# The gated convolution's input projection: every pair of tiles from the fourth block on by seven products, and the sixth product moved to fourth place

## The chip, the cores and the metric

One core of one Trainium2 chip runs the whole program once. The metric is the device time of that execution in microseconds (us). Engines by the profile's names: PE (TensorE matmul), PEld (its weight load), DVE (VectorE), ACT (ScalarE), POOL (GpSimd), SP (SyncE, which issues most DMAs here).

## The reference, cut to what matters

The program is one step of a four-layer decoder trunk for 512 prompt tokens and 8 sample tokens, 520 columns in all. The change touches the second layer alone, the short gated convolution:

```python
def shortconv_mixer(h, w_in, conv_w, w_out, buf):
    u = h @ w_in                           # 1024 -> 4 * 2048
    bg, cg, xb, z = jnp.split(u, 4, axis=-1)
    cx = cg * xb
    cpad = jnp.concatenate([buf.astype(cx.dtype), cx], axis=1)
    y = conv_w[0] * cpad[:, 0:T]
    for j in range(1, CONV_W):             # CONV_W = 3
        y = y + conv_w[j] * cpad[:, j:j + T]
    out = (bg * y * jax.nn.silu(z)) @ w_out
    return out, cpad[:, -(CONV_W - 1):]
```

All arrays are float32.

## The kernel before, in words

**Two halves of a float32.** TensorE is fed rounded operands, so each operand is held as a high part and a low part (value minus high part). A product takes three matmuls: high by high, high by low, low by high. For a weight tile `wf` of 128x1024 (128 outputs, all 1024 inputs) `high` (L255) is an ACT copy to `wh`. `low` (L257 to L264) is made in one of two ways. Mostly it is a DVE subtraction to `wl` (L264). For the first weight of a *moved* item (`Item.moved`, all of the convolution's weights except four) ACT writes the negated high part into `wl` (L260), and a DMA on POOL's queue adds the weight itself from HBM (L262).

**A plain tile** (`proj`, `mm6`): eight blocks of inputs, each with three matmuls (L334, L336, L338) on each of the two parts of the 520 columns.

**A pair by seven** (`seven`): two tiles, each cut into two halves of its inputs (a, b), against the activations cut in two halves of 260 columns, make eight block products; by sums of weights and of activations the same result comes from seven. Each product is twelve matmuls (L362 to L364). The weight sums `s1`, `s2`, `s4`, and a fourth that goes back into the second tile's `wf`, are four POOL instructions of 128x512 (L276 to L279, op "sum"); each of the three sums is split again into a high part `hs` (ACT) and a low part `ls` (DVE). The activations' sums are made once for the stage. Results are put together from PSUM by DVE adds: L380 (u2), L389 (u3), L393 (two halves at once), L372 (last quarter), and by ACT copies (L377, L386).

The order of a pair's products on PE is 11, T2, T1, then the seventh product "22" of the *previous* pair (`last`, run by `flush`, L384), then 21, T3, T4. So a pair's own last result and what hangs on it (`done`) come in the window of the pair or plain tile after it. r1 and r6 (the PSUM places) are used twice in a pair: 11 then 21, T2 then T3.

**The blocks.** The stage has 16 blocks j of four tiles: xb and cx (w_b 32+j and 16+j), bg and z (w_b j and 48+j). Blocks 0 to 2 are plain. From block 3 (`NPLAIN`) on, the first pair (xb, cx) goes by seven; the second pair (bg, z) goes by seven in even blocks and as two plain tiles in odd ones (`paired`). The `done` of a first pair multiplies cx by xb (L1109), and then runs the convolution: an ACT scaling (L1071), DVE L1076 to L1079, and two small POOL copies (L1067, L1068). The `done` of a second pair is a Silu on ACT and L1115 on DVE; in a plain block the same is L1126 and an ACT call. L1083, the product with the gate, is issued a little later from a side stream (`gate`).

**What sets the order.** The order is written by hand (`manual_schedule`): the order in which the program issues instructions is the order on each engine. Weights are made ahead of their use by a plan. `plan` lists items (a tile, or a pair), and `due` gives each step of an item (load, load2, sum, high, low, high2, low2, and the s parts) a due time on a planned clock, in which a plain tile costs 5.76 and a pair 10.08. It counts on 4 slots each for `wf`, `wh` (with `wl`) and `hs` (with `ls`): `take` gives the time at which a slot comes free. While the matmuls are written, `pump` issues each step once the planned clock has passed its due time. A pair's products pump 1.44 each.

Of the kernel before, what the change touches and what calls it, by code (L numbers as in the profile page):

```python
# [39 lines left out]
NPLAIN = 3  # L40
# [13 lines left out]

def paired(j):

    return 0 if j < NPLAIN else 2 - j % 2


def plan():  # L60
# [25 lines left out]
    for j in range(16):  # L86
        for n, q in enumerate(((2, 1), (0, 3))):
            keys = [("w_b", 16 * u + j) for u in q]
            if n < paired(j):
                out.append(Item(*keys, cost=10.08))  # L90
            else:
                out.extend(Item(key) for key in keys)
# [21 lines left out]
def due(items):  # L114

    ops, t, seq = [], 0.0, 0
    slots = {"wf": [0.0] * FBUFS, "wh": [0.0] * HBUFS, "hs": [0.0] * SBUFS}

    def take(tag, until):
        free = slots[tag]  # L120
        at = min(free)
        free.remove(at)
        free.append(until)
        return at

    def at(time, i, op):
        nonlocal seq
        ops.append((time, seq, i, op))
        seq += 1
        return time  # L130

    for i, it in enumerate(items):
        it.begin = t
        if len(it.keys) == 1:
            ld = min(slots["wf"])
            sp = at(max(ld, take("wh", t + (it.life or it.cost))), i, "high")
            low = at(sp + 1.3, i, "low")
            at(take("wf", low + 2) - 0.01, i, "load")
        else:
            ld, ld2 = sorted(slots["wf"])[:2]  # L140
            one = at(max(ld, ld2, t - 12.8), i, "sum")
            h1 = at(max(ld, take("wh", t + 5.76), t - 14.4), i, "high")
            h2 = at(max(ld2, take("wh", t + 10.08), one + 6.6), i, "high2")
            low1 = at(h1 + 1.3 if it.moved else max(h1 + 1.3, one + 3), i, "low")
            low2 = at(max(h2 + 1.3, one + 3), i, "low2")
            at(take("wf", max(low1, one + 7) + 1) - 0.01, i, "load")
            at(take("wf", low2 + 3) - 0.01, i, "load2")
            for n, need, until in (("2", t - 6.8, t + 2.88), ("1", t - 4.8, t + 4.32), ("4", t - 2.0, t + 17.3)):
                h = at(max(take("hs", until), need, one + 3), i, "high" + "s" + n)
                at(h + 0.6, i, "lows" + n)  # L150
        t += it.cost
    return sorted(ops)
# [42 lines left out]
class Net:  # L195
# [145 lines left out]
    def seven(self, keys, B, dst, done):  # L341

        nc = self.nc
        mm = nc.tensor.matmul
        t = self.item(*keys)
        a, b = slice(0, 512), slice(512, 1024)
        r1, r6, v = self.aux()[:, :HALF], self.aux()[:, :HALF], self.psum()  # L350
        r4, r5 = v[:, :HALF], v[:, 512 : 512 + HALF]
        part = lambda n, cols=slice(0, 512): (t["h" + n][:, cols], t["l" + n][:, cols])
        halves = self.act(), self.act()
        s1, u2, u3 = halves[0][:, :HALF], halves[0][:, HALF:], halves[1][:, :HALF]
        add = nc.vector.tensor_add

        def product(out, w, name, start):
            for k in range(4):
                c = slice(k * P, (k + 1) * P)
                hi, lo = B[name][k]  # L360
                go = {} if start else {"skip_group_check": True}
                mm(out, w[0][:, c], hi, start=start and k == 0, stop=False, **go)  # L362
                mm(out, w[0][:, c], lo, start=False, stop=False, **go)  # L363
                mm(out, w[1][:, c], hi, start=False, stop=k == 3, **go)  # L364

        def step():
            self.pump(1.44)
            self.tick()

        def last():  # L370
            product(r5, part("s4"), "22", False)
            add(dst[0][:, HALF:], r5, u2)  # L372
            done()
            step()

        product(r1, part("1", a), "11", True)
        nc.scalar.activation(s1, r1, AF.Copy)  # L377
        step()
        product(r6, part("s2"), "T2", True)
        add(u2, r6, s1)  # L380
        step()
        product(r5, part("s1"), "T1", True)
        step()
        self.flush()  # L384
        product(r1, part("1", b), "21", False)
        nc.scalar.activation(dst[0][:, :HALF], r1, AF.Copy)  # L386
        step()
        product(r6, part("2", a), "T3", False)
        add(u3, r6, s1)  # L389
        step()  # L390
        product(r4, part("2", b), "T4", True)
        pair = lambda x, n: x.rearrange("p (u c) -> p u c", u=2)[:, :, :n]
        add(pair(dst[1], HALF), pair(v, HALF), u3.unsqueeze(1).broadcast_to([P, 2, HALF]))  # L393
        step()
        self.pend = last
# [6 lines left out]
    @staticmethod  # L402
    def part(ps, j, m=P):

        n = PARTS[j].stop - PARTS[j].start
        if isinstance(ps, tuple):
            return ps[j][:m, :n]
        return ps[:m, BASE + PARTS[j].start : BASE + PARTS[j].stop]
# [643 lines left out]
    def conv(self, h, lay):  # L1052
# [4 lines left out]
        with ExitStack() as st:  # L1057
# [45 lines left out]
            def block(j):  # L1103
                xb, cx, z = (self.act() for _ in range(3))
                bg = self.act() if paired(j) > 1 else None
                c = []

                def first():
                    nc.vector.tensor_mul(cx, cx, xb)  # L1109
                    c.extend(taps(j, cx))  # L1110
                    conv(j, cx, *c)

                def second():
                    nc.scalar.activation(z, z, AF.Silu)
                    nc.vector.tensor_mul(c[0], bg, c[0])  # L1115
                    self.gate.gens.append(times(c[0], z))

                self.seven((("w_b", 32 + j), ("w_b", 16 + j)), self.sums, (xb, cx), first)
                if j == 15:
                    self.gate.drain()  # L1120
                    self.gate.gens.extend(parts(n) for n in range(4))
                if paired(j) > 1:
                    self.seven((("w_b", j), ("w_b", 48 + j)), self.sums, (bg, z), second)
                else:
                    ps = self.proj("w_b", j, a=h)
                    nc.vector.tensor_mul(c[0], ps, c[0])  # L1126
                    ps = self.proj("w_b", 48 + j, a=h)
                    nc.scalar.activation(z, ps, AF.Silu)
                    self.gate.gens.append(times(c[0], z))
# [557 lines left out]
```

## Time and profile before

| | us |
|---|---|
| median of three runs | 2155.67 |
| lowest and highest | 2151.12 and 2155.94 |
| the profiled execution | 2155.09 |
| its span, first to last instruction | 2153.3 |
| PE busy in the span | 2129.6 (99%) |
| DVE, ACT, POOL busy | 1383.3, 898.8, 395.2 |

The span lies 1.8 us below the time of the same execution. The convolution's pairs by seven run from about 655 to 945 us in the trace. In that stretch the granted clock is 1.00 throughout, which is the upper level, 2.4 GHz. A window of a pair is the time from its first matmul to that of what comes after it. The examples below are neighbouring windows: 745.65 to 755.71 (the second pair of an even block), 755.71 to 765.77 (the first pair of the odd block after it), 765.77 to 779.54 (that block's two plain tiles, with the flushed product among them), and 779.54 to 788.16 (the next block's first pair, which has nothing to flush).

### The profile page before, as it was taken

What the parts mean: (1) busy time and instruction counts of PE and PEld (TensorE: products, weight loads), DVE (VectorE), ACT (ScalarE), POOL (GpSimd) and SP (SyncE); (2) the same over time, 40 slices, a digit from 0 to 9 for tenths busy, and PEclk for the clock granted to TensorE, in tenths of its full rate; (3) what the DMA queues carried; (4) which work ended last, traced back from release to release, by engine and by line L of the source; (5) the groups of instructions that cost most, each with busy time, mean ns of one, the idle gap of its engine ahead of it and who ended that gap; (6) DMA issues with size and microseconds to landing.
All of it is one profiled execution on the core that took longest, in us unless ns stands there. A gap on an engine that the chain in (4) does not pass through costs nothing.

```text
span 2153.3 us, 42675 instructions
## 1 busy us (share of the span) xinstructions
PE 2129.6 (99%) x17560; PEld 2111.6 (98%) x17560; DVE 1383.3 (64%) x3064; ACT 898.8 (42%) x1434; POOL 395.2 (18%) x487
## 2 busy tenths in 40 slices
PE   8999999999999999999999999999999999999998
PEld 8999999999999999999999999999999999999998
DVE  7677767653565766751478787777867466666434
ACT  6544444432355554554333333333334342222223
POOL 1111110100035545521014223222220000000000
PEclk9999999999999999999999999999999999999999
DMA  4644454322257666678343555555544332323321
GB/s 164 193 177 143 154 182 165 99 95 93 89 140 165 159 169 164 157 198 188 88 136 120 162 193 190 185 173 165 199 169 156 98 114 93 98 90 99 119 79 50
DMA packets 112951, 305.22 MB, mean 142 GB/s; under 512 B 34260, under 2 KB 38612, under 8 KB 110708
## 3 DMA queue, kind: packets, MB, share of 16 engines
q1 hardware_dynamic: 104404, 272.54, 38.9%
q0 software_dynamic: 8208, 29.89, 7.8%
q8 instruction: 138, 2.26, 0.4%
q14 instruction: 57, 0.47, 0.1%
q10 hardware_dynamic: 144, 0.06, 0.0%
HBM read 279.63 MB, written 22.82 MB: 140 GB/s over the span
## 4 chain that ended last, share of the span: by engine, by line
PE 83%; DVE 6%; DMA 4%; issue 2%; ACT 2%; POOL 2%; SPq 0%; POOLq 0%; DVEq 0%; ACTq 0%
PE ps L334 23%; PE ps L338 23%; PE ps L336 23%; DMA wl<-w_b 2%; PE ax L1334 1%; PE ax L334 1%; PE ax L338 1%; PE ax L336 1%; DVE wl L264 1%; PE ax L364 1%; PE ax L362 1%; PE ax L363 1%; ACT wh L255 1%; PE ax L943 1%; PE ps L362 1%
## 5 line engine op out<-in xcount | busy, mean ns | idle before, releaser
L334 PE MATMUL ps<-hi,wh 128*128 128x256 f32 x4672 | 963.1, 287 | 1.8 <-DVE a L485 0.8
L338 PE MATMUL ps<-hi,wl 128*128 128x256 f32 x4672 | 939.5, 282 | 2.3 <-DMA wl<-w_b 2.3
L336 PE MATMUL ps<-lo,wh 128*128 128x256 f32 x4672 | 939.2, 282 | 0.1
L334 PEld LDWEIGHTS ps<-hi,wh 128*128 128x128 f32 x4672 | 725.8, 188 | 7.5 <-issue 1.4
L338 PEld LDWEIGHTS ps<-hi,wl 128*128 128x128 f32 x4672 | 723.4, 188 | 3.5 <-DMA wl<-w_b 3.3
L336 PEld LDWEIGHTS ps<-lo,wh 128*128 128x128 f32 x4672 | 725.3, 188 | 0.3 <-DVE lo L800 0.3
L264 DVE TENSOR_TENSOR wl<-wf,wh 128x1024 fp32r<-128x1024 f32 x287 | 364.2, 1272 | 167.3 <-ACT wh L255 163.8
L255 ACT ACTIVATE wh<-wf 128x1024 fp32r<-128x1024 f32 x344 | 360.8, 1053 | 157.2 <-issue 92.0
L1211 POOL TENSOR_TENSOR a<-a,a 32x520 f32<-32x520 f32 x48 | 68.9, 1436 | 296.1 <-ACT a L502 98.9
L627 DVE TENSOR_TENSOR x<-ps,x 128x520 f32<-128x520 f32 x32 | 22.4, 699 | 121.7 <-PE ps L338 121.6
L489 ACT ACTIVATE a<-a 128x520 f32<-128x520 f32 x42 | 26.8, 639 | 155.2 <-DVE a L485 155.1
L502 ACT ACTIVATE a<-ps 128x520 f32<-128x520 f32 x42 | 47.3, 1127 | 99.0 <-PE ps L338 72.5
L1212 POOL TENSOR_TENSOR a<-a,a 32x520 f32<-32x520 f32 x48 | 65.3, 1360 | 122.1 <-DVE a L1210 112.6
L466 ACT ACTIVATE hi<-x 128x520 fp32r<-128x520 f32 x32 | 20.5, 640 | 156.3 <-DVE x L627 156.3
L264 DVE TENSOR_TENSOR ls<-a,hs 128x512 fp32r<-128x512 f32 x57 | 65.4, 1158 | 12.1 <-ACT hs L255 11.9
L485 DVE TENSOR_TENSOR a<-ps,a 128x520 f32<-128x520 f32 x85 | 58.9, 693 | 20.8 <-PE ps L338 17.4
L649 DVE TENSOR_TENSOR a<-ax,a 128x256 f32<-128x256 f32 (+1 forms) x62 | 23.7, 424 | 72.5 <-ACT a L647 72.5
L1237 ACT ACTIVATE S<-S,nmx 128x128 f32<-128x128 f32 (+1 forms) x96 | 40.0, 417 | 65.8 <-DVE nmx L1234 65.5
L459 DVE CUSTOM_DVE_ANT_0 kc<-kc,qb 128x128 f32<-128x128 f32 (+1 forms) x192 | 54.3, 340 | 13.7 <-DMA kc<-kc 13.7
L262 POOL DMA_DIRECT2D wl<-w_b x41 | 36.3, 885 | 144.5 <-ACT wl L260 139.1
L260 ACT ACTIVATE wl<-wh 128x1024 fp32r<-128x1024 f32 x57 | 60.1, 1058 | 1.4
L1499 POOL COPY pool_p<-xpad 128x15 f32<-128x15 f32 x16 | 3.1, 196 | 300.7 <-DVE xpad L485 300.7
(344 smaller groups left out, 2924.4 us busy)
## 6 DMA issues: line engine op xcount, KB each, us to landing
wf<-w_c SPq DMA_DIRECT2D x80, 512.0 KB
wf<-w_a SPq DMA_DIRECT2D x64, 512.0 KB
wf<-w_b SPq DMA_DIRECT2D x64, 512.0 KB
wl<-w_b POOLq DMA_DIRECT2D x41, 512.0 KB, 7.1
wf<-w_pg SPq DMA_DIRECT2D x32, 512.0 KB
wf<-w_d SPq DMA_DIRECT2D x32, 512.0 KB
pb<-scr_p SPq DMA_DIRECT2D x8, 1292.0 KB
Ci<-C_in SPq DMA_DIRECT2D x16, 512.0 KB
```

The source lines that it names most:

```text
L255: nc.scalar.activation(t["h" + k], t["w" + k], AF.Copy)
L260: nc.scalar.activation(t["l1"], f(t["h1"]), AF.Copy, scale=-1.0)
L264: nc.vector.tensor_sub(t["l" + k], t["w" + k], f(t["h" + k]))
L334: mm(out[j], wh, a[0][:, PARTS[j]], start=start, stop=False)
L336: mm(out[j], wh, a[1][:, PARTS[j]], start=False, stop=False)
L338: mm(out[j], wl, a[0][:, PARTS[j]], start=False, stop=stop)
L362: mm(out, w[0][:, c], hi, start=start and k == 0, stop=False, **go)
L459: self.nc.vector.tensor_tensor_reduce(junk, a, b, 1.0, 0.0, ALU.mult, ALU.add, out)
L485: nc.vector.tensor_mul(dst[:, :T], ps, self.r)
L502: nc.scalar.activation(dst, split(ps), AF.Copy)
L1211: nc.gpsimd.tensor_mul(b[:32], t[:32], cs[0])
L1212: nc.gpsimd.tensor_mul(a[:32], a[:32], cs[1])
```

## The change

Four edits. `paired` gives 2 for every block from the fourth on, so that in the seven odd blocks 3, 5, ... 15 bg and z are made by `seven` too (19 pairs become 26). In `seven`, the product T4, which was the last of the six, is issued right after the flush; the two DVE adds L389 and L393 then both stand behind T3. The plan keeps the pair's first weight in its slot for 8.64 instead of 5.76, since product 21, its last reader, now comes later. And the low part of a moved single tile is planned at the time of its high part, not 1.3 behind it.

```diff
 def paired(j):
-    return 0 if j < NPLAIN else 2 - j % 2
+    return 0 if j < NPLAIN else 2
...
         if len(it.keys) == 1:
             ld = min(slots["wf"])
             sp = at(max(ld, take("wh", t + (it.life or it.cost))), i, "high")
-            low = at(sp + 1.3, i, "low")
+            low = at(sp if it.moved else sp + 1.3, i, "low")
...
-            h1 = at(max(ld, take("wh", t + 5.76), t - 14.4), i, "high")
+            h1 = at(max(ld, take("wh", t + 8.64), t - 14.4), i, "high")
...
         self.flush()
+        product(r4, part("2", b), "T4", True)
+        step()
         product(r1, part("1", b), "21", False)
         nc.scalar.activation(dst[0][:, :HALF], r1, AF.Copy)
         step()
         product(r6, part("2", a), "T3", False)
         add(u3, r6, s1)
-        step()
-        product(r4, part("2", b), "T4", True)
         pair = lambda x, n: x.rearrange("p (u c) -> p u c", u=2)[:, :, :n]
         add(pair(dst[1], HALF), pair(v, HALF), u3.unsqueeze(1).broadcast_to([P, 2, HALF]))
```

POOL's queue before, in the middle of the stage; the names are `wl` for a low weight part that a DMA completes, `wf` for a loaded weight, `a` for a sum or an activation:

```order
L262 DMA wl_8337<-w_b 128x1024
L276 TENSOR_TENSOR a_8353<-wf_8230 128x512
L277 TENSOR_TENSOR a_8354<-a_8353,wf_8186 128x512
L278 TENSOR_TENSOR wf_8230<-wf_8186,wf_8230 128x512
L279 TENSOR_TENSOR a_8355<-wf_8186,a_8354 128x512
L1067 COPY cv_p<-a_8248 128x2
L1068 COPY cv_s<-a_8248 128x8
L262 DMA wl_8460<-w_b 128x1024
L262 DMA wl_8520<-w_b 128x1024
L262 DMA wl_8593<-w_b 128x1024
L276 TENSOR_TENSOR a_8610<-wf_8478 128x512
```

The same queue now, in the same part of the stage:

```order
L262 DMA wl_8378<-w_b 128x1024
L1067 COPY cv_p<-a_8249 128x2
L1068 COPY cv_s<-a_8249 128x8
L276 TENSOR_TENSOR a_8486<-wf_8358 128x512
L277 TENSOR_TENSOR a_8487<-a_8486,wf_8318 128x512
L278 TENSOR_TENSOR wf_8358<-wf_8318,wf_8358 128x512
L279 TENSOR_TENSOR a_8488<-wf_8318,a_8487 128x512
L262 DMA wl_8515<-w_b 128x1024
L276 TENSOR_TENSOR a_8619<-wf_8495 128x512
L277 TENSOR_TENSOR a_8620<-a_8619,wf_8455 128x512
```

The three DMAs in a row (one for a pair, two for plain tiles) are gone: every sum is followed by one DMA and every DMA by a sum, with the two small copies between them in every second window.

DVE's queue before, at the seam between an even block and the odd one after it:

```order
L264 TENSOR_TENSOR ls_9541<-a_9403,hs_9524 128x512
L380 TENSOR_TENSOR a_9553<-ax_9551,a_9553 128x260
L372 TENSOR_TENSOR a_9298<-ps_9416,a_9417 128x260
L1115 TENSOR_TENSOR a_9479<-a_9298,a_9479 128x520
L389 TENSOR_TENSOR a_9554<-ax_9551,a_9553 128x260
L1083 TENSOR_TENSOR a_9297<-a_9479,a_9297 128x520
L393 TENSOR_TENSOR a_9546<-ps_9552,a_9554 128x520
L372 TENSOR_TENSOR a_9545<-ps_9552,a_9553 128x260
L1109 TENSOR_TENSOR a_9546<-a_9546,a_9545 128x520
```

And now, from the window of a block's second pair on:

```order
L264 TENSOR_TENSOR ls_9186<-a_9028,hs_9166 128x512
L1083 TENSOR_TENSOR a_8790<-a_8987,a_8790 128x520
L380 TENSOR_TENSOR a_9195<-ax_9193,a_9195 128x260
L264 TENSOR_TENSOR ls_9239<-a_9160,hs_9235 128x512
L372 TENSOR_TENSOR a_9058<-ps_9064,a_9065 128x260
L1109 TENSOR_TENSOR a_9059<-a_9059,a_9058 128x520
L1076 SCALAR_TENSOR_TENSOR a_9257<-a_9059,cols,a_9257 128x511
L1077 SCALAR_TENSOR_TENSOR a_9257<-a_9059,cols,a_9257 128x510
L1078 SCALAR_TENSOR_TENSOR a_9257<-cv_in,cols,a_9257 128x8
L1079 SCALAR_TENSOR_TENSOR a_9257<-cv_in,cols,a_9257 128x8
L264 TENSOR_TENSOR wl_9263<-wf_9035,wh_9237 128x1024
L264 TENSOR_TENSOR ls_9281<-a_9159,hs_9267 128x512
```

L1083 now stands in the same window as L1109, ahead of it, between the low part of s4 and that of s2; the low part of s1 (the last row) stands behind the whole convolution.

## Rows read from the trace of the kernel before

**Rows 1.** The page: busy time by engine, granted clock in slices, chain by engine.

```profile
PE 2129.6 (99%) x17560; PEld 2111.6 (98%) x17560; DVE 1383.3 (64%) x3064; ACT 898.8 (42%) x1434; POOL 395.2 (18%) x487
...
PEclk9999999999999999999999999999999999999999
...
PE 83%; DVE 6%; DMA 4%; issue 2%; ACT 2%; POOL 2%; SPq 0%; POOLq 0%; DVEq 0%; ACTq 0%
```

**Rows 2.** Waits of PEld, 640 to 960 us: total us, times, longest us.

```profile
PEld ps L338 <- DMA wl<-w_b: 3.3, 5, 0.8
```

**Rows 3.** Timeline of PE: start us, us, line, operation, idle before.

```profile
755.71 0.28 PE L362 MATMUL ax<-hi,wh 128*128 128x260 f32 x1
...
765.77 0.40 PE L334 MATMUL ps<-hi,wh 128*128 128x256 f32 x2
...
766.95 0.51 PE L338 MATMUL ps<-hi,wl 128*128 128x256 f32 x2 [0.54 <-DMA wl<-w_b]
767.29 0.40 PE L334 MATMUL ps<-hi,wh 128*128 128x256 f32 x2
767.53 0.40 PE L336 MATMUL ps<-lo,wh 128*128 128x256 f32 x2
...
779.54 0.28 PE L362 MATMUL ax<-hi,wh 128*128 128x260 f32 x1
```

**Rows 4.** Windows: busy PE, PEld, DVE, ACT, POOL, then clock, DMA share, GB/s.

```profile
745.65:755.71 10.06, 10.06 (x86) 10.06 (x85) 7.49 (x8) 4.79 (x9) 7.11 (x7) 1.00 0.60 154
755.71:765.77 10.06, 10.06 (x86) 10.06 (x85) 6.02 (x12) 7.22 (x10) 1.75 (x2) 1.00 0.81 200
765.77:779.54 13.77, 13.23 (x110) 13.03 (x109) 10.17 (x13) 5.25 (x7) 8.09 (x9) 1.00 0.59 137
779.54:788.16 8.62, 8.62 (x74) 8.62 (x73) 6.31 (x7) 5.32 (x8) 5.34 (x4) 1.00 0.69 174
```

**Rows 5.** DVE's groups, 655 to 945 us: busy us, mean ns of one | idle before.

```profile
L264 DVE TENSOR_TENSOR ls<-a,hs 128x512 fp32r<-128x512 f32 x57 | 65.4, 1158 | 12.1 <-ACT hs L255 11.9
L264 DVE TENSOR_TENSOR wl<-wf,wh 128x1024 fp32r<-128x1024 f32 x19 | 24.0, 1264 | 1.1 <-ACT wh L255 1.1
...
L393 DVE TENSOR_TENSOR a<-ps,a 128x520 f32<-128x520 f32 x19 | 13.3, 700 | 8.2 <-PE ps L364 7.6
...
L1115 DVE TENSOR_TENSOR a<-a,a 128x520 f32<-128x520 f32 x6 | 4.2, 700 | 0.2
```

**Rows 6.** Timeline of DVE in the first window and just behind it.

```profile
746.47 2.63 DVE L264 TENSOR_TENSOR ls<-a,hs 128x512 fp32r<-128x512 f32 x1
...
751.96 0.42 DVE L372 TENSOR_TENSOR a<-ps,a 128x260 f32<-128x260 f32 x1
752.41 1.35 DVE L1109 TENSOR_TENSOR a<-a,a 128x520 f32<-128x520 f32 x1
...
757.54 0.68 DVE L264 TENSOR_TENSOR ls<-a,hs 128x512 fp32r<-128x512 f32 x1
```

**Rows 7.** Timeline of POOL, the same windows.

```profile
746.32 0.91 POOL L262 DMA_DIRECT2D wl<-w_b  x1 [3.42 <-ACT wl L260]
746.93 1.61 POOL L276 TENSOR_TENSOR a<-wf 128x512 f32<-128x512 f32 x1
748.62 1.62 POOL L277 TENSOR_TENSOR a<-a,wf 128x512 f32<-128x512 f32 x1
750.20 1.28 POOL L278 TENSOR_TENSOR wf<-wf,wf 128x512 f32<-128x512 f32 x1
751.44 1.75 POOL L279 TENSOR_TENSOR a<-wf,a 128x512 f32<-128x512 f32 x1
...
757.77 0.89 POOL L262 DMA_DIRECT2D wl<-w_b  x1 [3.63 <-ACT wl L260]
```

**Rows 8.** Timeline of ACT: the copy behind product 21, and an `hs` part.

```profile
754.95 0.37 ACT L386 ACTIVATE a<-ax 128x260 f32<-128x260 f32 x1
...
757.26 0.62 ACT L255 ACTIVATE hs<-a 128x512 fp32r<-128x512 f32 x1
```

**Rows 9.** The DMAs of L262 by source line, whole program.

```profile
DMA to landing us min/median/max: 5.4/7.1/9.9
```

**Rows 10.** The chain of waits, 752 to 768 us: start, us, what.

```profile
757.77 9.13 DMA wl<-w_b
```

## The prediction

> **What bounds the kernel now.** I read the page first. PE is busy for 2129.6 of 2153.3 us, the clock stands at its upper level in every slice, and 83% of the chain of waits lies on PE [rows 1]. So time goes only where PE does less work, or where a wait of PE goes. Next I read the waits of PE in the convolution's stretch, because the change is there alone. The only one of size is a plain tile's low weight part, which a DMA of POOL's queue completes: five waits of PEld, 3.3 us in all [rows 2]. Then the timeline of PE, for what each form costs. The first window, a pair by seven, runs from one L362 to the next stretch's first matmul: 755.71 to 765.77, 10.06 us, seven products of 1.44 [rows 3]. The two plain tiles with one flushed product take 765.77 to 779.54, 13.77 us. In them one wait can be seen: L334 at 767.29 is the fourth group of matmuls, which at the pace of 0.24 (767.29 to 767.53) would have begun at 766.49, so 0.80 is lost [rows 3]. Last I read DVE, POOL and ACT in the same windows, since the change takes 1.5 us from PE in each odd block and gives these engines more to do in it [rows 4 to 8].
>
> **PE's work.** Without its wait and the flushed product the plain stretch is 13.77 - 0.80 - 1.44 = 11.53 us. A pair costs 10.06. Each of the seven odd blocks saves 1.47: 10.3 us. The plain tiles' waits lie in these same blocks and go with them, if nothing takes their place: 3.3 us [rows 2]. The best case is 13.6 us, or 2155.1 - 13.6 = 2141.5 on the clock of the profiled run, which stands 0.6 below the median of the three.
>
> **DVE and POOL.** Seven more pairs bring, each, four POOL sums and, on DVE, three `ls` parts (3 x 1.16), a `wl` (1.26), three small adds (0.42 each) and a double one (0.70) [rows 5, 6]; L1115 at 0.70 replaces an add of the same size. That is 6.7 us on DVE per odd block. The three windows and the next, which make up two blocks, hold 7.49 + 6.02 + 10.17 + 6.31 = 30.0 us of DVE work in 42.51 us now [rows 4]; with 6.7 more it is 36.7, in 4 x 10.06 = 40.2 us. DVE's share goes from 71% to 91%. Averages do not decide, though. What does is a deadline in one window.
>
> **The deadline.** An `ls` part alone takes 0.68, but the one at 746.47 took 2.63: it began 0.46 before POOL's L276, and ended at 749.10, 0.56 after L276 ended (748.54). L1109 (0.70 for a form like L1115's) began in L279 and took 1.35, to 753.76, 0.57 after L279's end at 753.19 [rows 5 to 7]. L372, with one operand in PSUM, takes 0.42 even in L279 [rows 6]. So each POOL op of a sum lets about one DVE op with two SBUF operands through, at its own end plus 0.56. In the window from 745.65, POOL's sum began at +1.28, its four ops ended at about +2.9, +4.6, +5.8 and +7.5, and L1109 went through behind the last of them, at +8.1. From there a fixed row follows (the scaling on ACT, L1076 to L1079, a `wl`, then the `ls` of s1), and this `ls` ended at 758.22, +12.57 [rows 6]. T1 is the third product of the next window and its third matmul is the first to read it: 10.06 + 2 x 1.44 + 0.24 = +13.18. So 0.6 us are left today.
>
> What changes: the order has one sum and one DMA by turns, the sum behind the DMA. That DMA cannot go before the weight slot is free, which is at the end of the product 21 two pairs earlier. A pair now has 21 as its sixth product (with the flush), so its end is 8.64 behind that pair's start, 11.5 before the start of the pair for which the DMA loads. From the copy behind 21 (754.95) to the DMA (757.77) ACT's row took 2.82 [rows 7, 8]. With 0.2 from PE's end to ACT, and at most one `hs` of 0.62 more ahead, the DMA goes 8.5 to 7.9 before its pair; I take 8.0, or +2.1 in the window. The sum then begins at +2.7 (0.61 behind its DMA, as at 746.32 and 746.93 [rows 7]), 1.4 later than in the window shown. Three operations that suffer from it, `ls` of s4, L1083 (new here) and `ls` of s2, stand ahead of L1109. If all three are caught behind POOL, L1109 goes through behind the fourth op again, at 8.1 + 1.4 = +9.5, the `ls` of s1 ends at +14.0, and T1 waits 0.8. If L1083 misses a slot, L1109 falls behind the sum's end and adds its own 0.7: 1.5. If `ls` of s4 and L1083 get away before the sum begins, L1109 goes through behind the third op, at about 9.5 - 1.7 = +7.8, and the `ls` of s1 ends at +12.3, in time. The price is so 0 to 1.5 for each of 12 seams between a block's second pair and the next first one.
>
> I take caught, because it feeds itself. A DVE that ends its window late begins the next `ls` of s4 late, and the margin to stay clear is small: that `ls` began at +0.82 in the window shown, and two operations of 0.68 behind it end at +2.2, half a microsecond before POOL's sum. DVE at 91%, without what further caught operations add, has little pause in which to catch up. At first it is free, so of 12 seams I count 10 or 11, and 1.1 us each, nearer to 0.8 than to 1.5: 11.5 us.
>
> On who goes first the Trainium skill speaks against this. Its page "SBUF — State Buffer", section "Who interferes with whom", says that a DVE operation with two SBUF inputs and a GpSimd operation that reads SBUF share a port pair as an exclusive lock, and that whichever began first keeps it for its whole instruction. The trace agrees on which operations are touched (L372 is not), but not on the order: the `ls` at 746.47 began first and still took 2.63 [rows 6]. By the rule that `ls` would have ended at 747.15, POOL would have waited, and the rival "clear" below would be the outcome.
>
> **The accumulating DMA.** PE needs a pair's first low part at its third matmul, 0.24 in. The DMA that goes 8.0 before may so take 8.2. Over the program such DMAs took 5.4 to 9.9, median 7.1 [rows 9]. A pair loads three weights in 10.06 us from now on (two `wf`, one `wl`). The nearest window is the first: the same 154 GB/s, one DMA at 746.32, and its pair at 755.71 began without a wait. The other end is 9.13 at 757.77, in a window with 200 GB/s [rows 4, 10]. I take 7.2 to 8.2 and nothing.
>
> **The rest.** T4 in fourth place reads the second tile's low part 1.44 earlier, at +5.8. In the window from 755.71 that `wl` stands directly ahead of the `ls` that starts at 757.54, +1.8; DVE hides it with 4 us to spare. The adds L389 and L393 come together behind T3; L393 reads two PSUM halves which the next pair does not write, so nothing waits on them but the `hs` and `ls` behind them on DVE. The low parts of single moved tiles are planned 1.3 sooner on ACT, where high and low already stand next to each other: nothing. At the output projection's first tiles a late DMA may cost 0 to 1 once.
>
> **Sum.** 2155.1 - 10.3 - 3.3 + 11.5 = 2153.0. The two ends of the same sum: 2141.5 with no price at the seams, and 2155.1 - 13.6 + 12 x 1.5 + 1 = 2160.5.
>
> **Rivals.** *Clear*: DVE gets `ls` of s4 and L1083 away before POOL's sum, as the rule of the page would have it, or the jam is rare. For it: 0.6 us are free today, u2 and L380 get more room since T3 comes later, and a wait of PE gives DVE as much time to catch up. Against it: the 2.63 of an `ls` that had begun first. Up to four jammed seams: 0 to 5 us back, 2141.5 to 2147. *Slow loads*: two `wf` and the `wl` come out in a burst, as at 757.77, in every pair. Then each `wl` takes 9.1 instead of 8.2, PE waits 0.9 at the head of each of 26 pairs, 23 us, and the time is 2155.1 - 13.6 + 23 = 2165. It decides from a landing of 9.0: 0.8 x 26 - 13.6 is 7 us on the slow side. For it: the same three transfers stood together in the trace; against it: it was the window with the most bytes, and the one like the new ones shows 7.2 or less. *Nothing new on PE*: were the odd blocks' pairs not formed, the time would stay; the order shows them formed, so it gets no chance.
>
> **How the numbers follow.** Jam, with 2149 to 2161: 0.50. Clear, 2141.5 to 2149: 0.36. Slow loads, above 2162: 0.14. A difference under 0.3% (6.5 us) is about what a measurement of this kernel cannot tell from none. Around 2155.7 that is 2149.2 to 2162.1, so the three cases are the three chances: faster 0.36, same 0.50, slower 0.14. The likeliest case gives 2153. Its own range is 2149 to 2161; the 8 in 10 must take in the clear case too, so 2141 to 2161, which leaves out the slow loads.
>
> **What would show it.** Right: a pair's products without a wait at 10.06, and at most of the seams a wait of PE at L364 or of PEld for `ls` from DVE, 0.8 to 1.5 each, in the third product of a first pair; L1083 and `ls` of s4 each ending about 0.56 behind a POOL op; POOL's sum from about +2.7. Clear: no such wait, `ls` of s1 ending before +13.2. Slow loads: PE waits at L364 for `wl` from a DMA at the third matmul of the pairs, and landings of 9 or more. It is wrong altogether if PE waits somewhere that I gave no price: for `hs`, for an `aux` place behind L391, or in the output projection behind.

## The result: 33 us slower

The changed kernel takes 2187.95 us (median of 4 runs, 2183.18 to 2191.78), the kernel before 2154.73 beside it: ratio 1.0157, 95% interval 1.0142 to 1.0172. The forecast was no change, 2153, and a range up to 2161. The profiled execution took 2191.78 with a span of 2189.9, 36.6 longer than before. It is the slowest of the four and the one with the lowest mean granted clock, 0.987; the other three have 0.991 or 0.992.

First the page of the profile after, its busy times; the columns are those of [rows 1].

```profile
PE 2142.4 (98%) x17476; PEld 2122.4 (97%) x17476; DVE 1450.8 (66%) x3120; ACT 911.2 (42%) x1462; POOL 442.0 (20%) x508
```

PE has 84 instructions fewer than in [rows 1] and is busy 12.8 us *longer*. So some matmuls became slower, which a wait alone cannot do. Next the waits of PE in the stage, 600 to 1000 us: engine, who waited for whom, total us, times, longest.

```profile
PE ps L364 <- DVE ls L264: 22.4, 12, 1.9
PE ps L362 <- DVE a L393: 2.0, 1, 2.0
```

The plain tiles' waits for a `wl` DMA [rows 2] are gone, and nothing of that sort has come. In their place stand twelve waits for an `ls` part, one at each seam between a block's second pair and the next first pair, and one for L393 at the stage's last pair. Here is one seam on PE, with T1's first two matmuls, the pause, and what follows (start us, us, line, operation, idle before):

```profile
742.93 0.29 PE L362 MATMUL ps<-ha,hs 128*128 128x260 f32 x1
743.05 0.28 PE L363 MATMUL ps<-la,hs 128*128 128x260 f32 x1
745.19 0.39 PE L364 MATMUL ps<-ha,ls 128*128 128x260 f32 x1 [1.86 <-DVE ls L264]
745.42 0.29 PE L362 MATMUL ps<-ha,hs 128*128 128x260 f32 x1
...
746.05 0.42 PE L363 MATMUL ps<-la,hs 128*128 128x260 f32 x1
```

The third matmul should have begun at 743.17 and began at 745.19: 2.02 late. And from 745.83 on matmuls take 0.42 and follow each other at 0.22, where they took 0.28 and 0.12. The windows of the same piece tell why; columns as in [rows 4], the granted clock is the third number from the end:

```profile
742.93:745.19 2.26, 0.40 (x4) 0.19 (x2) 2.26 (x4) 1.58 (x2) 1.27 (x2) 1.00 0.41 40
745.19:745.83 0.64, 0.64 (x4) 0.64 (x5) 0.61 (x2) 0.00 (x0) 0.00 (x0) 0.91 0.61 166
745.83:749.47 3.64, 3.64 (x20) 3.64 (x19) 1.92 (x4) 1.27 (x2) 1.76 (x2) 0.55 1.02 257
749.47:760.00 10.53, 10.53 (x90) 10.53 (x89) 8.60 (x11) 4.83 (x7) 5.65 (x4) 1.00 0.60 159
```

After the pause the clock is granted at its lower level, 1.2 GHz, for most of 3.6 us (0.55 with the edges), then at 2.4 GHz again. So one seam costs 2.02 of waiting and some 1.6 behind it, nearly all of it slow matmuls: T1 and the two products behind it begin at 742.93 and end at 750.91, 7.98 us, where three products take 4.32. That is 3.66, and the twelve seams lie between 3.64 and 3.68. The sum: -13.6 (the prediction's saving) + 12 x 3.66 + 3.7 (the last pair, below) = +34.0, of the 36.6 by which the spans differ. Of the other 2.6, some 1.4 lie behind the stage: PE stands still for 2.3 us at L1418 in both kernels, and in the changed kernel's profile (from 1230 on) the granted clock falls behind it, in that of the kernel before (at 1194) it does not. The last 1.2 I place nowhere; the first pair begins at 673.70 in both profiles.

**What DVE and POOL do in that seam.** First DVE, then POOL, from the profile after:

```profile
731.95 0.68 DVE L264 TENSOR_TENSOR ls<-a,hs 128x512 fp32r<-128x512 f32 x1
732.55 0.69 DVE L1083 TENSOR_TENSOR a<-a,a 128x520 f32<-128x520 f32 x1
...
736.39 0.70 DVE L1109 TENSOR_TENSOR a<-a,a 128x520 f32<-128x520 f32 x1
737.89 1.38 DVE L1076 SCALAR_TENSOR_TENSOR a<-a,cols,a 128x511 f32<-128x511 f32 x1 [0.80 <-ACT a L1071]
739.31 1.67 DVE L1077 SCALAR_TENSOR_TENSOR a<-a,cols,a 128x510 f32<-128x510 f32 x1
740.90 1.26 DVE L1078 SCALAR_TENSOR_TENSOR a<-cv_in,cols,a 128x8 f32<-128x8 f32 x1
742.20 1.21 DVE L1079 SCALAR_TENSOR_TENSOR a<-cv_in,cols,a 128x8 f32<-128x8 f32 x1
743.33 1.21 DVE L264 TENSOR_TENSOR wl<-wf,wh 128x1024 fp32r<-128x1024 f32 x1
744.46 0.68 DVE L264 TENSOR_TENSOR ls<-a,hs 128x512 fp32r<-128x512 f32 x1
```

```profile
732.08 0.89 POOL L262 DMA_DIRECT2D wl<-w_b  x1 [1.67 <-ACT a L377]
737.16 0.18 POOL L1067 COPY cv_p<-a 128x2 f32<-128x2 f32 x1 [4.20 <-DVE a L1109]
737.28 0.19 POOL L1068 COPY cv_s<-a 128x8 f32<-128x8 f32 x1
737.44 1.29 POOL L276 TENSOR_TENSOR a<-wf 128x512 f32<-128x512 f32 x1
...
742.10 1.28 POOL L279 TENSOR_TENSOR a<-wf,a 128x512 f32<-128x512 f32 x1
743.33 0.88 POOL L262 DMA_DIRECT2D wl<-w_b  x1
```

POOL stands idle for 4.20 us in front of two copies of 2 and 8 columns that wait for DVE's L1109. The sum is queued behind them. So it starts at the moment at which DVE starts the convolution's four operations, and holds each of them up: L1076 1.38, L1077 1.67, and the two of 8 columns 1.26 and 1.21, where one of the last kind takes 0.21 alone (e3, below). The `ls` of s1, last in this row, ends at 745.14. L1109 itself, and the `ls` of s4 and L1083 ahead of it, were through without a delay.

### The profile page after: what moved, and what is told of

Its sections match the earlier page's. It is cut to its first block, busy times and chain, and to the rows that moved or that the text cites. A ratio compares the mean times of both kernels' runs of the same rounds, so it can differ in the third digit from the quotient of the medians.

```text
span 2189.9 us, 42589 instructions
## 1 busy us (share of the span) xinstructions
PE 2142.4 (98%) x17476; PEld 2122.4 (97%) x17476; DVE 1450.8 (66%) x3120; ACT 911.2 (42%) x1462; POOL 442.0 (20%) x508
## 4 chain that ended last, share of the span: by engine, by line
PE 85%; DVE 8%; issue 3%; ACT 2%; DMA 1%; POOL 1%; SPq 0%; ACTq 0%; POOLq 0%; DVEq 0%
PE ps L334 22%; PE ps L338 22%; PE ps L336 22%; PE ps L364 2%; PE ps L362 2%; PE ps L363 2%; DVE wl L264 1%; PE ax L1334 1%; PE ax L364 1%; PE ax L362 1%; PE ax L363 1%; PE ax L336 1%; PE ax L338 1%; PE ax L334 1%; DVE a L1077 1%
## 5 line engine op out<-in xcount | busy, mean ns | idle before, releaser
L334 PE MATMUL ps<-hi,wh 128*128 128x256 f32 x4448 | 918.3, 288 | 2.0 <-DVE a L485 1.0
L338 PE MATMUL ps<-hi,wl 128*128 128x256 f32 x4448 | 895.6, 283 | 0.1
L336 PE MATMUL ps<-lo,wh 128*128 128x256 f32 x4448 | 895.4, 283 | 0.2
L334 PEld LDWEIGHTS ps<-hi,wh 128*128 128x128 f32 x4448 | 692.4, 189 | 7.4 <-issue 1.5
L336 PEld LDWEIGHTS ps<-lo,wh 128*128 128x128 f32 x4448 | 691.2, 189 | 0.6 <-DVE lo L1136 0.3
L338 PEld LDWEIGHTS ps<-hi,wl 128*128 128x128 f32 x4448 | 689.5, 189 | 0.4 <-DMA wl<-w_bo 0.3
L264 DVE TENSOR_TENSOR wl<-wf,wh 128x1024 fp32r<-128x1024 f32 x294 | 387.2, 1320 | 167.2 <-ACT wh L255 164.5
L255 ACT ACTIVATE hs<-a 128x512 fp32r<-128x512 f32 x78 | 48.8, 625 | 26.4 <-PE ax L363 23.5
L364 PE MATMUL ax<-hi,wl 128*128 128x260 f32 x208 | 59.0, 284 | 0.0
```

The source lines that it names most:

```text
L255: nc.scalar.activation(t["h" + k], t["w" + k], AF.Copy)
L264: nc.vector.tensor_sub(t["l" + k], t["w" + k], f(t["h" + k]))
L334: mm(out[j], wh, a[0][:, PARTS[j]], start=start, stop=False)
L336: mm(out[j], wh, a[1][:, PARTS[j]], start=False, stop=False)
L338: mm(out[j], wl, a[0][:, PARTS[j]], start=False, stop=stop)
```

## The experiments

Times are medians, with the kernel before on the same chip beside it.

| run | what it is | us | before | ratio, 95% interval |
|---|---|---|---|---|
| e1_pairs_only | all pairs by seven, T4 last, plan of before | 2163.00 | 2155.66 | 1.0032 (1.0021 to 1.0044) |
| e2_t4_only | T4 fourth and new plan, odd blocks plain | 2157.65 | 2155.66 | 1.0013 (1.0003 to 1.0022) |
| e3_copies_act | changed kernel, copies on ACT | 2150.99 | 2155.66 | 0.9975 (0.9966 to 0.9984) |
| e4_conv_late | changed kernel, L1076 to L1079 later | 2164.31 | 2155.66 | 1.0044 (1.0026 to 1.0062) |
| e5_fill14 | changed kernel, pause filled with matmuls | 2172.96 | 2154.87 | 1.0087 (1.0071 to 1.0102) |
| e6_small_late | changed kernel, L1078 and L1079 later | 2177.23 | 2154.87 | one run |
| e7_pairs_copies | e1 with the copies on ACT | 2165.27 | 2154.87 | 1.0051 (1.0036 to 1.0065) |
| e8_best | e3, last pair reordered | 2150.47 | 2154.87 | 0.9977 (0.9967 to 0.9987) |
| e9_h1_576 | changed kernel, one number of the plan | 2159.21 | 2154.59 | 1.0023 (1.0013 to 1.0033) |
| e10_sum16 | changed kernel, sum planned sooner | 2151.71 | 2154.59 | 0.9989 (0.9980 to 0.9998) |
| e11_last | e3, T1's quarter of the last pair copied out | 2148.83 | 2154.59 | 0.9976 (0.9967 to 0.9985) |
| e12_last_free | e11, T4 of the last pair in its own PSUM tile | 2146.08 | 2155.21 | 0.9965 (0.9952 to 0.9977) |

### One part at a time

**e1_pairs_only.** The kernel before with the first edit alone:

```diff
-    return 0 if j < NPLAIN else 2 - j % 2
+    return 0 if j < NPLAIN else 2
```

> One part alone: every pair from the fourth block on by seven, but T4 stays last in its pair and the plan is the one of before. Here POOL's queue has the sum behind the accumulating DMA of the same pair again, and that DMA waits for a weight slot. Theory 1 (the sum of the changed kernel falls on the convolution's four DVE operations because the new order puts it directly behind the two small copies that wait for L1109): no waits of 1.9 us on the low part of s1, and the full saving of 13.6 us less about 4 at the last pair: 2142 to 2148. Theory 2 (DVE is simply too full with two pairs in every block, whatever the order): waits at the same seams, 1 us or more each, 2160 to 2190.

The time and the waits lie in theory 2's range, and theory 1's 2142 to 2148 is missed. But the seams wait less than in the changed kernel, eleven of them, and in another way. PE's wait, then DVE, then POOL at one seam:

```profile
PE ps L364 <- DVE ls L264: 13.9, 11, 1.3
```

```profile
748.58 2.58 DVE L264 TENSOR_TENSOR ls<-a,hs 128x512 fp32r<-128x512 f32 x1
751.08 1.78 DVE L1083 TENSOR_TENSOR a<-a,a 128x520 f32<-128x520 f32 x1
...
753.13 1.43 DVE L264 TENSOR_TENSOR ls<-a,hs 128x512 fp32r<-128x512 f32 x1
...
754.93 1.34 DVE L1109 TENSOR_TENSOR a<-a,a 128x520 f32<-128x520 f32 x1
```

```profile
748.39 0.88 POOL L262 DMA_DIRECT2D wl<-w_b  x1 [3.17 <-ACT wl L260]
749.01 1.59 POOL L276 TENSOR_TENSOR a<-wf 128x512 f32<-128x512 f32 x1
...
753.97 1.74 POOL L279 TENSOR_TENSOR a<-wf,a 128x512 f32<-128x512 f32 x1
756.34 0.18 POOL L1067 COPY cv_p<-a 128x2 f32<-128x2 f32 x1 [0.63 <-DVE a L1109]
```

This is the jam of the prediction, with the very operations that it named: `ls` of s4, L1083 and `ls` of s2 each caught behind a POOL op, L1109 behind the fourth. T1 takes 2.98 instead of 1.44 there, 1.54 a seam, and the granted clock stays at 1.00 behind these shorter pauses. Whether DVE is too full, or held up by POOL's order, this run does not tell; e3 and e10 do. So the forecast described the kernel with T4 last, not the one with T4 in fourth place. In the changed kernel POOL's queue is another: the copies, which stand behind the sum here, stand ahead of it there.

**e2_t4_only.** The changed kernel with `paired` as before.

> The other parts alone: T4 in fourth place and the new plan, but the odd blocks' second pairs stay plain. Theory 1: in odd blocks the sum stands behind plain tiles' DMAs; where in even blocks it stands behind the copies the convolution could be hit, but there the next window's deadline has the plain tiles' room behind it. So 2150 to 2158, no change. Theory 2 (DVE too full): also no change, 2150 to 2158. A rival that the move of T4 by itself costs time, through a result that is put together later, gives 2162 or more.

2.0 us slower, at the edge of what can be told from no change. PE's waits in the stage are 1.1 us for two DMAs at the head of pairs, and a few of 0.3 and less. In its profile the clock also falls behind the pause at L1418, outside the stage, as it does not in that of the kernel before. The move of T4 alone costs nearly nothing. It takes both parts together.

### The place in POOL's queue

**e3_copies_act.** The changed kernel; the two copies go from POOL to ACT, behind L1071:

```diff
-                nc.gpsimd.tensor_copy(po[:, j], cx[:, NP - 2 : NP])
-                nc.gpsimd.tensor_copy(so[:, j, 1], cx[:, NP:T])
...
                 nc.scalar.activation(yc, cx, AF.Copy, scale=w2)
+                nc.scalar.activation(po[:, j], cx[:, NP - 2 : NP], AF.Copy)
+                nc.scalar.activation(so[:, j, 1], cx[:, NP:T], AF.Copy)
```

> The changed kernel with the two small copies L1067 and L1068 on ACT, behind L1071, so that POOL's sum no longer stands behind operations that wait for L1109. Theory 1: the sum begins when its loads have landed, some 2.5 us sooner than now, two of its four operations are over before L1076 starts, and the wait at a seam falls from 2.0 to about 0.5, with no fall of the granted clock behind it: 2146 to 2155. Theory 2 (DVE too full): the seams keep 1.5 us or more, 2175 to 2190.

37 us back, and 4.7 us below the kernel before. PE's waits of the stage:

```profile
PE ps L362 <- DVE a L393: 2.0, 1, 2.0
PE ax L364 <- DMA wl<-w_b: 1.4, 3, 0.7
```

Not one wait for an `ls` is left, better than the 0.5 that I expected. DVE and then POOL at a seam:

```profile
732.66 0.90 DVE L1076 SCALAR_TENSOR_TENSOR a<-a,cols,a 128x511 f32<-128x511 f32 x1 [0.80 <-ACT a L1069]
733.60 1.67 DVE L1077 SCALAR_TENSOR_TENSOR a<-a,cols,a 128x510 f32<-128x510 f32 x1
735.19 0.21 DVE L1078 SCALAR_TENSOR_TENSOR a<-cv_in,cols,a 128x8 f32<-128x8 f32 x1
```

```profile
728.04 1.51 POOL L276 TENSOR_TENSOR a<-wf 128x512 f32<-128x512 f32 x1 [0.53 <-DMA wf<-w_b]
...
732.97 1.74 POOL L279 TENSOR_TENSOR a<-wf,a 128x512 f32<-128x512 f32 x1
```

The sum is now released by its load, not by L1109, and is over when the convolution's second operation runs. The work of every engine is the same but for two small copies. That DVE is too full in the changed kernel, whatever the order, is thereby refuted.

**e10_sum16.** Is it the order, or that POOL has two operations less? The changed kernel with the sum planned 3.2 sooner, all else in its order:

```diff
-            one = at(max(ld, ld2, t - 12.8), i, "sum")
+            one = max(ld, ld2, t - 12.8)
+            at(max(ld, ld2, t - 16), i, "sum")
```

> The changed kernel with the sum, and it alone, planned 3.2 sooner (16 instead of 12.8 ahead of its pair): it then stands ahead of the two copies in POOL's queue, and behind the DMA of the pair before; all other operations keep their order. Theory 1: as with the copies on ACT, no waits at the seams, only the last pair's pause is left: 2147 to 2154. Rival (moving the copies helped because it took two operations from POOL, not because of the order): waits of 1 us or more at the seams stay, 2165 or more.

The order. The copies stay on POOL, behind the sum now, and the twelve waits are gone: one of 0.4 is left. It gains 2.9 against the kernel before, less than e3, because the first pair's sum now falls on the last plain tiles, where PE waits for L486 up to 3.1 us (two waits, 3.9), and the clock falls with the longer of them.

**e9_h1_576.** Which of the four edits put the copies ahead of the sum? Here one number of the plan is put back:

```diff
-            h1 = at(max(ld, take("wh", t + 8.64), t - 14.4), i, "high")
+            h1 = at(max(ld, take("wh", t + 5.76), t - 14.4), i, "high")
```

> The changed kernel with one number put back: the plan frees the pair's first weight slot after 5.76, not 8.64; T4 stays in fourth place. By that number alone POOL's queue goes back to sum, copies, DMA, next sum, so that the sum no longer stands behind the copies, but behind its own pair's DMA, as with T4 last. Theory 1 (the place in POOL's queue decides, T4's place does not): no pause of 2.0 and no fall of the clock; waits at the seams of 1.0 to 1.5 as with T4 last: 2155 to 2166. If T4's place by itself were to blame, the 2.0 and the fall would stay, 2180 to 2192.

With that the queue reads sum, copies, DMA, next sum, as with T4 last, and the sum waits for its DMA. 2159.21: twelve waits, 11.0 us, none over 1.0, and no fall of the clock in the stage. So it was the plan's number that decided, through the turn of sum and DMA in a queue that is served in order, and not T4's place in itself. That T4's place helps a little is seen against e1: T1 takes 2.70 at a seam, 1.26 over, instead of 1.54.

**e7_pairs_copies.** The counter-test: e1 with the copies on ACT.

> T4 last and the plan of before, all pairs by seven, and the two small copies on ACT: the same move of the copies as in the run before that took the waits away, on the other order of products. Here the sum stands behind the DMA, not behind the copies, so theory 1 says the copies hold nothing up: the seams keep their 1.45 us, 2158 to 2166. If it falls to 2153 or less, the place of T4 is not needed, and the copies alone are the cause.

As expected nothing: eleven waits, 13.7 us, 1.3 the longest, as in e1. Where the copies stand behind the sum they hold nothing up, and moving them brings nothing.

### The convolution's operations

**e4_conv_late.** The changed kernel; `conv(j, cx, *c)` is put on a list that is worked off at the end of the pair, behind L393.

> The changed kernel with the convolution's four DVE operations (L1076 to L1079) issued at the end of the pair, behind L393, instead of at once behind L1109; the low part of s1 then stands ahead of them. The work is the same. Theory 1: no wait at the seams, the granted clock stays at 1.00, and only the last pair's wait is left: 2143 to 2150. Theory 2 (DVE too full): the delay only moves to the next low part, waits of 1 us or more in most windows, 2165 or more.

Half of it, and 2164.31 is outside the 2143 to 2150. The `ls` waits are gone, but there are new ones, for the accumulating DMA at the head of the second pairs:

```profile
PE ax L364 <- DMA wl<-w_b: 11.7, 11, 1.6
```

ACT and POOL show where the DMA was held. On ACT, then POOL (this kernel's L1070 is the first small copy, L1112 the product that was L1109):

```profile
735.54 1.06 ACT L260 ACTIVATE wl<-wh 128x1024 fp32r<-128x1024 f32 x1
```

```profile
732.00 1.11 POOL L1070 COPY cv_p<-a 128x2 f32<-128x2 f32 x1 [5.47 <-DVE a L1112]
...
733.21 1.28 POOL L276 TENSOR_TENSOR a<-wf 128x512 f32<-128x512 f32 x1
...
737.95 1.74 POOL L279 TENSOR_TENSOR a<-wf,a 128x512 f32<-128x512 f32 x1
739.64 0.88 POOL L262 DMA_DIRECT2D wl<-w_b  x1
```

The weight was ready for its DMA at 736.60; the DMA went at 739.64, behind a sum that stood behind copies that waited for DVE. In the changed kernel the same DMA also goes behind that sum, 3.3 us after its block's first pair has begun (4.8 here), but there the seam costs 3.66 before the second pair begins, and the DMA has that much longer to land. The copies therefore press on two deadlines, one over DVE, one over the DMA; with the sum ahead of them or without them on POOL (e10, e3) both are met.

**e6_small_late.** Only the two operations of 8 columns go behind L393.

> The changed kernel with the two operations of 8 columns (L1078, L1079; 0.22 us each alone) issued behind L393. Theory 1 (each DVE operation with two SBUF operands takes one POOL operation of the sum, however small it is): the wait of T1 falls by some 1.2 us, from 2.0 to 0.8, with no fall of the clock; the accumulating DMA, which stands behind the sum, is then what comes late, by up to 1 us at the second pairs: 2156 to 2168 in all. Rival (they cost by their size): the wait falls by 0.45, stays at 1.5 or more, 2165 to 2185.

The wait fell from 1.9 to 1.6, by 0.24 us, and the clock did not fall in the stage. By its ranges that is the rival (1.5 or more, 2165 to 2185), and theory 1's 0.8 is missed; but what the row shows is neither. The freed POOL ops were not free time for DVE: the `wl` and the `ls` moved up into them and were caught themselves (the `wl` took 2.32, the `ls` 1.76, at 738.16 and 740.40). The last operation of the row still ends some 0.5 behind the sum, whatever stands ahead of it. PE also waits ten times, 6.5 us in all, for the accumulating DMA at the head of the second pairs. The time, 2177.23, is one run.

### The clock

**e5_fill14.** The changed kernel with 14 matmuls by zeros ahead of T1's third matmul:

```diff
                 mm(out, w[0][:, c], lo, start=False, stop=False, **go)
+                for _ in range(14 if name == "T1" and k == 0 and keys[0][1] >= 36 else 0):
+                    mm(out, self.zero, hi, start=False, stop=False, **go)
```

> The changed kernel with 14 matmuls by a tile of zeros (each adds nothing) ahead of the third matmul of T1 in the first pair of blocks 4 to 15: PE works through 1.7 of the 2.0 us for which it stands still there. Nothing else moves. Theory 1 (half of a seam's 3.66 us is the clock that falls behind the pause): the matmuls behind the seam stay at 0.12 us, a seam costs 2.0, and 12 x 1.65 = 20 us come back: 2164 to 2172. Rival (the slow matmuls come from the queue or the weight loads behind a late operand, not from the clock and the pause): they stay at 0.22, 2184 to 2192.

15 us less than the changed kernel by the medians, 1 us outside the band that I gave; from the first pair to L1418 the two profiles differ by 19.9, 18.4 of them at the seams and 1.5 at the last pair, whose pause brought the clock down in the changed kernel's profile and not in this one. The other three executions of the changed kernel have a higher mean clock than the profiled one, so they had less to give back. The seam on PE:

```profile
741.75 1.86 PE L365 MATMUL ps<-ha,zero 128*128 128x260 f32 x14
743.76 0.39 PE L366 MATMUL ps<-ha,ls 128*128 128x260 f32 x1 [0.15 <-DVE ls L264]
743.99 0.28 PE L362 MATMUL ps<-ha,hs 128*128 128x260 f32 x1
```

The operand is as late as ever, but PE is not idle while it waits, and the matmuls behind it take 0.28: the granted clock stays at 1.00. A seam costs 2.13 instead of 3.66 (T1 with its filling takes 3.57, where 1.44 is normal). So 1.53 of the 3.66 is the clock, which falls behind a pause of PE and not where PE works through it; it is not something that a late operand does to the matmuls behind it.

### The last pair

**e8_best, e11_last, e12_last_free.** In the changed kernel and in e3 the stage's last product, "22" of the last pair, is flushed at once behind T3, and waits 2.0 us for L393, which reads the same PSUM tile. In the changed kernel's profile the clock falls behind it (0.62 in 980.5 to 985.0). In e3's it does not, behind the same pause; the matmul that waits, and the window from 942 on with the clock third from the end:

```profile
941.47 0.39 PE L362 MATMUL ps<-hi,hs 128*128 128x260 f32 x1 [1.97 <-DVE a L393]
```

```profile
942.00:945.00 3.00, 3.00 (x27) 2.98 (x27) 1.69 (x4) 2.97 (x5) 0.32 (x1) 1.00 1.06 299
```

The expectations of the three tries that follow overlook this, and count slow matmuls that e3 does not have there. All three build on e3 and change the last pair only. e8 issued T3 ahead of 21 and T4:

> The changed kernel with the copies on ACT from block 3 on, and the very last pair with T3 ahead of 21 and T4 and its double add in two, so that its last product does not wait for L393. Against the run with the copies alone this should take away the last pair's 2.0 us and the slow matmuls behind it, 3 to 4 us: 2145 to 2149.

Nothing won: T3 now waited 2.5 us for its own reader of before, the add of u2 (L388 in that kernel). e11 had ACT copy T1's quarter out of PSUM ahead of time:

> The changed kernel with the copies on ACT from block 3 on and, in the very last pair alone, T1's quarter copied by ACT out of PSUM, so that the last product can add to its place without waiting for L393. Against the run with the copies alone this takes away the last pause of 2.0 us and the slow matmuls behind it: 3 to 4 us less, 2146 to 2149. If the clock behind that pause cost nothing, 2 us less.

The 2.0 stayed, on the add that reads T4's half: the wait goes by the whole PSUM tile, not by the half. What e11 gains over e3 is within the runs, and its 2148.83 lies in the range given for another reason than the one given: the pause is still there. e12 gave T4's result a tile of its own:

> The kernel before this one in the list (copies on ACT, T1's quarter copied out in the last pair), with the last pair's T4 result in a PSUM tile of its own. In the kernel of that earlier run the last product still waited 2.0 us, on the add that reads T4's half of the same PSUM tile (its line 398). With a tile of its own nothing is left to wait for: the 2.0 us and the slow matmuls behind it, 1.5, go: 2144 to 2147, 3 to 4 below it. If another result is late there, the pause stays and the time with it, 2148 to 2151.

2146.08, and the largest of PE's waits in 600 to 1000 us are now these:

```profile
PE ps L334 <- DVE a L494: 0.8, 1, 0.8
PE ax L366 <- DMA wl<-w_b: 0.4, 1, 0.4
```

It is 9.1 us faster than the kernel before, and 42 than the changed one. From e11 to e12 the gain against the kernel before went from 5.8 to 9.1: 3.4 us by the medians, with intervals that overlap. By the profiles 2.7 lie between the first pair and L1418, where the pause of 2.0 has gone; e11's clock had stayed at 1.00 behind it, so there were no slow matmuls to take away. Another 1.3 lie behind, from L1418 on, where the clock fell in e11's profile and not in e12's. DVE is busy for 93% of the time in its pairs, as this window shows (DVE is the third busy time), and PE does not wait:

```profile
700.00:720.00 20.00, 20.00 (x169) 20.00 (x169) 18.62 (x23) 12.16 (x20) 16.61 (x12) 1.00 0.67 158
```

## Why the prediction was wrong, step by step

- **PE's work, 13.6 us.** Right. The waits of [rows 2] went, and with the new waits taken away e12 keeps 9.1 of it in time, with PE 11.5 us less busy than in [rows 1].
- **The deadline.** Right. What PE waits for is the `ls` of s1, at the third matmul of T1 of a first pair, at 12 of 12 seams.
- **The start of the sum: here the prediction failed.** "The sum then begins at +2.7 (0.61 behind its DMA ...)" passes over the two copies L1067 and L1068. They are in the order shown ahead of the prediction, between the DMA and the sum; I named them and gave them no price. They wait for L1109, POOL is served in order, and so the sum began at 737.44, 2.6 before the next pair's start at 740.04, and not 7.4 before it. Nor could L1109 go through behind a sum that itself waits for L1109. In the kernel before the copies stood behind the sum (L1067 ran at 753.82, L279 at 751.44), and so held nothing up there.
- **Who is caught.** Wrong for this kernel, as a consequence: `ls` of s4, L1083 and L1109 went clear, and the four operations behind L1109, which I had as a fixed row of known length, were caught. e1 shows the forecast jam, at the upper end of its price.
- **The price of a seam, 0 to 1.5 (I took 1.1, at 10 or 11 of 12).** It measured 2.13 without the clock (e5), at all twelve, outside my bounds, since four operations were caught behind L1109 and none ahead.
- **The clock, no term at all.** In the profiled execution each of these pauses added 1.53 us by matmuls at 1.2 GHz (3.66 against e5's 2.13). I read PEclk at 1.00 in the kernel before and carried it over; the waits in its stage were 0.8 at most [rows 2]. By itself this term is 12 x 1.53 = 18.4 us, half of the 36.6 by which that profile is longer; in the other three executions, with a higher mean clock, it was smaller. Without it the two other misses give 2155.1 - 13.6 + 12 x 2.13 + 2 = 2169, already out of the range.
- **"Nothing waits on" L391 and L393.** Wrong once: the last pair's own flush does, 2.0 us, and in the changed kernel's profile the clock besides. I had looked at the next pair, and the last one has none.
- **The accumulating DMA.** Right for the changed kernel (no wait in its stage), and nearly so where the seams are gone (1.4 in e3, 0.3 in e10, 0.4 in e12). But with the copies ahead of the sum it is the next in line (11.7 in e4, 6.5 in e6), for a reason I did not have: not its landing time, but its place behind the sum.
- **The rivals.** *Clear* was right as a mechanism, for the kernels with the copies out of the way: 2146 to 2151 against 2141.5 to 2149, so e3 lies just outside. *Slow loads* did not occur. The case that came about, slower through DVE and POOL, I had bounded at 2161.
- **Who goes first on the shared port.** Against the Trainium skill's rule I held that the `ls` at 746.47 began ahead of L276 and still took 2.63. That reading overlooked a row: POOL was not idle then. It had begun L262, the issue of a DMA, at 746.32, with the sum directly behind it [rows 7]; in e1 it is the same (748.39 and 748.58). Where POOL was idle, the DVE operation that had begun first was not held up. DVE, then POOL, in the changed kernel:

```profile
723.26 0.68 DVE L264 TENSOR_TENSOR ls<-a,hs 128x512 fp32r<-128x512 f32 x1
```

```profile
723.61 1.47 POOL L276 TENSOR_TENSOR a<-wf 128x512 f32<-128x512 f32 x1 [3.22 <-DMA wf<-w_b]
```

Here the `ls` kept its 0.68, and L276 took 1.47, where it took 1.27 behind an `ls` that was nearly over (747.07 and 747.63). It was so in all 117 such cases of the fourteen profiles: a subtraction or product of DVE with two SBUF operands, begun between 600 and 1000 us with POOL idle, that met an operation of POOL before its end. L1083 in e3 is among them. Of e6's ten operations of 8 columns that met a sum in this way one, begun only 0.04 ahead, was held up. In the 117 the traces agree with the rule of the Trainium skill ("SBUF — State Buffer", "Who interferes with whom") that the first to start keeps the port pair. Of 90 that began while POOL issued a DMA and met an operation of POOL behind it, 55 were held up, to between 2.3 and 2.6 us, and 35 were not; what decides there is open.

## What to carry to other kernels

A tiny operation in an in-order queue is a gate: what it waits for becomes what everything behind it waits for, so each new order has to be walked past every entry, with the question of what releases it. A plan's number that seems to concern one resource (here the life of a weight slot) can swap two entries of another engine's queue; compare the queues row by row, and price the rows that changed places. And a pause of PE is to be priced twice, without and with a fall of the clock behind it, since the same pause had either outcome here.

## What the runs showed of the hardware that I had not expected

- **The clock's fall.** In the profiled execution of the changed kernel the waiting matmul came 2.02 us late at each of twelve seams (PE idle for 1.9), and the granted clock went to 1.2 GHz between 0.35 and 1.12 us after PE had gone on, for most of 3.6 us. Where it came 1.44 late (e1, wait 1.3, eleven times) or 1.78 (e6, wait 1.6, twelve times) the clock stayed at 2.4 GHz, and also where PE worked through the pause on zeros (e5).
- **A pause's length alone does not decide it.** At the last pair PE stands still for 1.8 to 2.0 us in eight kernels: the clock fell behind that pause in three (the changed kernel, e1, e7) and stayed in five (e3, e5, e9, e10, e11). At L1418 of the kernel before, and at the same place in every kernel, there is a pause of 2.3 to 2.4; the clock fell with it in ten of the fourteen profiles, and not in the kernel before:

```profile
1194.12 0.22 PE L1418 MATMUL ax<-ident,sT 64*8 64x64 f32 x1 [2.35 <-DVE sT L459]
```

The twelve seams follow each other at equal distances, so they are one case repeated rather than twelve. The other three executions, with mean clocks of 0.991 to 0.992 against 0.987, must have had fewer falls. An estimate from these means is eight to ten, where the profiled one has fifteen within its span (one at its start, the twelve, the last pair, L1418). What else it takes for the clock to fall is not shown.

- **A DVE operation's size hardly matters while POOL sums.** Operations of 8 and of 511 columns with two SBUF operands took 1.21 to 1.67 alike, one for each POOL operation. Taking two of them out of the row (e6) gave back 0.24 us of waiting, not the 2.0 that the two had cost, because the next ones took their places.
